# Layer 0's output projection: half of its contraction by seven block products for two outputs at a time

## The chip, the cores and the metric

The kernel runs on one core of a Trainium2 chip. The metric is the device time of one execution in microseconds (us); lower is better. The times are those of the executions that were timed, and beside them stands one profiled execution, whose trace gives every row quoted here.

TensorE (PE in the rows) multiplies a 128x128 block of weights with a moving tile and adds into PSUM; the loads of weights have rows of their own (PEld). VectorE (DVE) and ScalarE (ACT) work on SBUF and PSUM. SyncE (SP) issues most of the DMAs, GpSimd (POOL) those that add to their destination.

## The reference, cut to what matters

One step of a two-layer trunk in float32 over 576 tokens (512 of a prompt, 64 of samples), model width 1024 and branch width 2048. Layer 0 is a gated short convolution:

```python
def short_conv_mixer(h, buf, w_in, conv_w, w_out):
    b_gate, c_gate, xa, z = jnp.split(h @ w_in, 4, axis=-1)
    u = c_gate * xa
    conv, new_buf = causal_dwconv(u, buf, conv_w)
    y = b_gate * conv * jax.nn.silu(z)
    return y @ w_out, new_buf
...
    x = x + out
```

The change concerns `y @ w_out` of layer 0, a contraction over 2048 to 1024 outputs, and the residual sum. Layer 1 (an mLSTM block with the same kind of output projection) and the final norm come after it.

## The kernel before, in words

Everything is kept transposed: an activation is a tile of 128 features by 576 tokens, so the model width is 8 such tiles (`KD`) and the branch width 16 (`NW`). The precision of float32 is kept by splitting: `split` (L162) makes from a tile a high part (a cast by ScalarE) and a low part (a subtraction by VectorE), and each product of a 128x128 weight block with a tile is three matmuls, high by high, high by low and low by high.

**Two ways to multiply.** The plain way, `gemm` (L252) over `products` and `step`, runs for each of 8 blocks of weights three matmuls over two pieces of the tokens, 256 and 320 wide (L235). One output over a contraction of 2048 is two chunks of weights: 2 x 8 x 3 x 2 = 96 matmuls.

The other way, `block_pair` (L325), takes two outputs over a contraction of 1024 as a 2x2 block product: the two outputs are the rows, the even and odd feature tiles the inner blocks, the two halves of the tokens (288 each, `HT`) the columns. It uses a scheme of Strassen's kind with seven products in place of eight. Each product is 4 pairs of feature tiles by 3 matmuls of 288 columns (L345), so a pair of outputs takes 7 x 12 = 84 matmuls, where the plain way takes 96. The inputs must be there as sums and differences of the halves: `forms` (L283, with `mixed`, L268) makes them from two feature tiles, in four subtractions and additions of half a tile and three and a half splits. The weights must be there as sums too: `block_weights` (L302) loads two chunks (`r1`, `r2`), and in layer 0 lets DMAs build two of the sums: `s1` is loaded by SP and then added to by a POOL DMA, and one block of `r1` is added onto `r2`; VectorE makes the third sum in two steps (L354 and L350). `parts_of` (L258) splits each of the seven weight blocks, 128x512, one cast on ScalarE (L264) and one subtraction on VectorE (L265); four buffers each for high and low parts let it run up to three products ahead. Some products go through ScalarE copies out of PSUM on their way (L357, L362, L365, L375).

`plain` (L425) is the plain way in the two token halves of a block pair, 8 x 3 x 2 = 48 matmuls for a chunk. Layer 1 uses `gemm_pair` (L440) for its value projection: seven block products for one half of the contraction, then `plain` for the other half of both outputs, into the same PSUM banks.

**Layer 0.** The loop over `f` (L606 to L666) makes the 16 tiles of the branch: two block pairs for each `f` from 2 on, the convolution and gates on VectorE, and at its end `split` of the result into `ya` (L664). Then come the eight outputs of the output projection (L674 to L681): `gemm` over both chunks, the residual tile `x` loaded by SP and added from PSUM, its store, the scaled split for layer 1 (`h2`) and the sum of squares.

**What orders the work.** The kernel is written for a tile framework: code order gives priorities, and a scheduler with a timeline of its own fixes the order on each engine at build time. Each engine then runs its queue in order. Tiles of one tag share a fixed number of slots: 70 for the activation tiles (`T`), 4 for raw weight chunks, 7 for the scratch tiles of layer 0 (`X`, L108: the sums `s1` and `s2`, and `pu` and `m5` of a block pair, and some convolution inputs), 4 PSUM banks for the blocks of pairs.

## Time and profile before

| | us |
|---|---|
| median of 3 executions (1655.06 to 1657.25) | 1655.9 |
| span of the profiled execution, first to last instruction | 1654.3 |
| PE busy | 1627.4 (98%) |
| PE's weight loads busy | 1548.7 (94%) |
| DVE busy | 1125.8 (68%) |
| ACT busy | 806.9 (49%) |
| POOL busy | 148.8 (9%) |

The profiled execution's own time is its span of 1654.3 us and the little that lies around it. The other three executions were only timed, so the 1.6 us between span and median is taken as what lies around a span. In the rows a time is in us from the start of the span. A row of the timeline gives start, length, engine, line of the code, operation, output and inputs, and in brackets the time that the engine sat idle before it with the instruction that ended the wait. A row of the stretches gives, for a window, the busy time and the number of instructions of each engine, TensorE's granted clock (1.00 is full), the busy share of the DMA engines and GB/s.

Layer 0's loop ends and its output projection begins near 375 us; the last of the eight residual sums is at 479 us.

### The profile page before, as it was taken

The page shows a single profiled execution, that of the slowest core. Times are in us where ns is not written, and L with a number is a line of the kernel's source. Part 1 is how long each engine was busy: PE and PEld are TensorE (multiplying, and loading weights), DVE is VectorE, ACT ScalarE, POOL GpSimd, SP SyncE. Part 2 cuts the span into 40 slices and gives each one's busy share as a digit, 9 for nine tenths or more (in the row PEclk, how much of TensorE's full clock was granted, in tenths as well). Part 3 has the DMA queues.
Part 4 walks back from the last instruction along what each step waited for, and adds up shares of the span by engine and source line. Part 5 has one row for each costly group of instructions (what it writes and reads, how often), then busy time and mean ns, then how long its engine had stood idle before and what let it go on. Part 6 is the DMA issues. An engine that isn't in the chain of part 4 may idle for free. (4 is left out here: it accounts for less than half of the span.)

```text
span 1654.3 us, 31177 instructions
## 1 busy us (share of the span) xinstructions
PE 1627.4 (98%) x12029; PEld 1548.7 (94%) x12029; DVE 1125.8 (68%) x2124; ACT 806.9 (49%) x1622; POOL 148.8 (9%) x295
## 2 busy tenths in 40 slices
PE   9999999999999999999999999999999998999998
PEld 9999999999999999999899989899898787989997
DVE  7988898885337976555966456446458658688775
ACT  5566666653324553434645344344345456556431
POOL 1111111110001000000111010110101000000000
PEclk9999999999999999999999999999999899999999
DMA  6476666654332434535434554454556587998992
GB/s 219 111 174 167 175 168 159 175 136 148 120 120 91 149 121 128 172 119 159 156 103 151 156 177 162 142 188 140 173 190 241 186 280 262 336 341 296 359 342 103
DMA packets 121893, 301.61 MB, mean 182 GB/s; under 512 B 12656, under 2 KB 35056, under 8 KB 121744
## 3 DMA queue, kind: packets, MB, share of 16 engines
q1 hardware_dynamic: 98320, 267.61, 48.7%
q0 software_dynamic: 8064, 14.68, 5.8%
q10 hardware_dynamic: 15360, 17.32, 3.1%
q8 instruction: 94, 1.54, 0.4%
q14 instruction: 55, 0.45, 0.1%
HBM read 235.91 MB, written 63.66 MB: 181 GB/s over the span
## 5 line engine op out<-in xcount | busy, mean ns | idle before, releaser
L345 PE MATMUL p<-hi,wh 128*128 128x288 f32 x1540 | 454.4, 297 | 3.9 <-ACT p L357 1.9
L345 PE MATMUL p<-lo,wh 128*128 128x288 f32 x1540 | 452.6, 294 | 0.0
L345 PE MATMUL p<-hi,wl 128*128 128x288 f32 x1540 | 450.7, 295 | 0.2 <-DVE wl L265 0.2
L345 PEld LDWEIGHTS p<-hi,wh 128*128 128x128 f32 x1540 | 288.5, 188 | 12.7 <-DVE ws L350 4.1
L345 PEld LDWEIGHTS p<-lo,wh 128*128 128x128 f32 x1540 | 289.0, 188 | 0.0
L345 PEld LDWEIGHTS p<-hi,wl 128*128 128x128 f32 x1540 | 287.9, 188 | 0.4 <-DVE wl L265 0.4
L264 ACT CAST wh<-wr 128x512 fp32r<-128x512 f32 (+1 forms) x298 | 171.4, 578 | 215.4 <-PE p L345 123.5
L265 DVE TENSOR_TENSOR wl<-wr,wh 128x512 fp32r<-128x512 f32 (+1 forms) x298 | 185.0, 635 | 94.9 <-ACT wh L264 92.5
L235 PE MATMUL acc<-hi,wh 128*128 128x256 f32 (+1 forms) x1072 | 233.4, 298 | 1.8 <-ACT xm L711 1.0
L235 PE MATMUL acc<-lo,wh 128*128 128x256 f32 (+1 forms) x1072 | 231.9, 297 | 0.0
L235 PE MATMUL acc<-hi,wl 128*128 128x256 f32 (+1 forms) x1072 | 231.7, 297 | 0.0
L264 ACT CAST wh<-ws 128x512 fp32r<-128x512 f32 (+1 forms) x201 | 114.8, 573 | 203.8 <-PE p L345 129.6
L215 ACT CAST wh<-wr 128x512 fp32r<-128x512 f32 x170 | 104.7, 619 | 201.2 <-PE acc L235 148.1
L235 PEld LDWEIGHTS acc<-hi,wh 128*128 128x128 f32 x1072 | 180.4, 190 | 7.4 <-issue 1.6
L216 DVE TENSOR_TENSOR wl<-wr,wh 128x512 fp32r<-128x512 f32 x170 | 116.7, 689 | 98.7 <-ACT wh L215 88.6
L235 PEld LDWEIGHTS acc<-hi,wl 128*128 128x128 f32 x1072 | 179.9, 190 | 1.6 <-issue 1.3
L235 PEld LDWEIGHTS acc<-lo,wh 128*128 128x128 f32 x1072 | 179.9, 190 | 0.6 <-issue 0.2
L265 DVE TENSOR_TENSOR wl<-ws,wh 128x512 fp32r<-128x512 f32 (+1 forms) x201 | 125.5, 630 | 68.7 <-ACT wh L264 68.0
L1236 DVE SCALAR_TENSOR_TENSOR c<-c,cols,r 128x512 f32<-128x512 f32 x128 | 91.5, 743 | 27.0 <-PE r L1235 24.9
L433 PE MATMUL p<-hi,wh 128*128 128x288 f32 x496 | 109.2, 300 | 0.0
L433 PE MATMUL p<-hi,wl 128*128 128x288 f32 x496 | 107.3, 295 | 0.0
L433 PE MATMUL p<-lo,wh 128*128 128x288 f32 x496 | 107.0, 295 | 0.0
(388 smaller groups left out, 2619.1 us busy)
## 6 DMA issues: line engine op xcount, KB each, us to landing
wr<-wts SPq DMA_DIRECT2D x222, 512.0 KB, 3.6
c<-cs SPq DMA_DIRECT2D x112, 512.0 KB, 5.8
cs_out<-c SPq DMA_DIRECT2D x64, 512.0 KB, 7.5
ws<-wts SPq DMA_DIRECT2D x28, 256.0 KB, 4.5
ws<-wts POOLq DMA_DIRECT2D x28, 256.0 KB, 4.7
wr<-wts POOLq DMA_DIRECT2D x28, 256.0 KB, 4.1
x<-xcs SPq DMA_DIRECT2D x20, 288.0 KB, 4.8
x<-xT SPq DMA_DIRECT2D x16, 288.0 KB, 4.3
```

The costliest lines, as they stand in the source:

```text
L215: last_act[0] = nc.scalar.copy(hi, raw[:, 4 * i:4 * i + 4, :]).ins
L216: nc.vector.tensor_tensor(lo, raw[:, 4 * i:4 * i + 4, :], hi.bitcast(F32), ALU.subtract)
L235: nc.tensor.matmul(acc[:, o:o + j - i], a[:, k % 4, :], x[:, i:j], start=(first and k == 0 and p == 0), stop=(last and k == 7 and p == 2))
L264: last_act[0] = nc.scalar.copy(hi, src).ins
L265: nc.vector.tensor_tensor(lo, src, hi.bitcast(F32), ALU.subtract)
L345: nc.tensor.matmul(bank_, a[:, j, :], x, start=(start and n + j + i == 0), stop=(n == len(groups) - 1 and j == len(g) - 1 and i == 2), ski ...
L433: nc.tensor.matmul(b, a[:, k % 4, :], x[:, t:t + HT], start=bool(start) and k == 0 and i == 0, stop=(k == n - 1 and i == 2), skip_group_ch ...
L1236: ins = nc.vector.scalar_tensor_tensor(ct[:, j, :], ct[:, j, :], dec[:, o + j:o + j + 1], r, ALU.mult, ALU.add).ins
```

## The change

The two halves of the projection's contraction change places in the weight array, so that an even chunk (64, 66, ...) now belongs to the tiles `ya[8]` to `ya[15]` and an odd one (65, 67, ...) to `ya[0]` to `ya[7]`; the even chunks are stored with their blocks in the order that the block products want. The tiles 8 to 15 are no longer split; they become four `forms`, the first made within the loop after `f == 12`, the other three between the first plain products. The projection then runs so:

1. the weights of the first pair of outputs are requested (`block_weights(64, 66)`);
2. for outputs 0 to 3, `plain_onto`: the plain half over `ya[0:8]`, 48 matmuls each, added to the residual tile;
3. the seven products for outputs 0 and 1, then for 2 and 3, added onto these tiles (the existing `add` path of `block_pair`);
4. for outputs 4 and 5, then 6 and 7, `gemm_pair` with the new `onto`: seven products, then the plain half of each output into the same banks, then the sums onto the residual tile.

Each pair requests the weights of the next one (`then`). The opening of layer 1's buffers (`load_buffers("C", "states1", 2)`) and the end of layer 0's way of making weight sums (`layer0[0] = False`) move behind the projection.

```diff
@@ block_pair @@
+            if onto:
+                tt(o12, o12, u, ALU.subtract)
+                plain(bx, bw, c1 + 1, xs, None)
+                tt(o11, bx, o11, ALU.add)
+                tt(o12, bw, o12, ALU.add)
+                tt(o22, o22, m5, ALU.subtract)
+                plain(by, bv, c2 + 1, xs, None)
+                tt(o21, by, o21, ALU.add)
+                tt(o22, bv, o22, ALU.add)
+                return
...
+        def plain_onto(chunk, xs, o):
+
+            ba, bb = block(), block()
+            plain(ba, bb, chunk, xs, True)
+            for b, t in ((ba, 0), (bb, HT)):
+                nc.vector.tensor_tensor(o[:, t:t + HT], b, o[:, t:t + HT], ALU.add)
...
-            ya.append(split(cv))
+            ya.append(split(cv) if f < 8 else cv)
+            if f in (12,):
+                fy.append(forms(ya[8], ya[9]))
...
-        load_buffers("C", "states1", 2)
-        layer0[0] = False
...
-        for m in range(KD):
-            acc = gemm(64 + 2 * m, 2, ya)
+        block_weights(64, 66)
+        firsts = []
+        for m in range(4):
             x = T(name="x")
             load(out=x, in_=io["xT"][m])
-            nc.vector.tensor_tensor(x, flat(acc), x, ALU.add)
-            store(out=x1s[m], in_=x)
-            h2.append(split(x, col("norm1", m)))
-            sumsq(ssq, x, m == 0)
+            firsts.append(x)
+            plain_onto(65 + 2 * m, ya[0:8], x)
+            if m < 3:
+                fy.append(forms(ya[10 + 2 * m], ya[11 + 2 * m]))
+        for m in range(0, KD, 2):
+            c1, c2 = 64 + 2 * m, 66 + 2 * m
+            then = (c1 + 4, c2 + 4) if m < KD - 2 else None
+            if m < 4:
+                pair = firsts[m:m + 2]
+                groups, _ = ahead_of.pop((c1, c2))
+                block_pair(c1, c2, fy, None, *pair, True, then=then, groups=groups)
+            else:
+                pair = [T(name="x") for _ in range(2)]
+                for i, x in enumerate(pair):
+                    load(out=x, in_=io["xT"][m + i])
+                gemm_pair(c1, c2, fy, ya[0:8], *pair, then=then, onto=True)
+            for i, x in enumerate(pair):
+                store(out=x1s[m + i], in_=x)
+                h2.append(split(x, col("norm1", m + i)))
+                sumsq(ssq, x, m + i == 0)
+        load_buffers("C", "states1", 2)
+        layer0[0] = False
...
+    aout = _chunks(f["a_w_out"][0])[:, ::-1]
...
+    blk = [c for c in range(8, 64) if c % 4 < 2 or c // 4 in SECOND] + list(range(64, 80, 2))
```

## The prediction

> **What bounds the kernel now.** First the page's table of engines.

> ```profile
> span 1654.3 us, 31177 instructions
> PE 1627.4 (98%) x12029; PEld 1548.7 (94%) x12029; DVE 1125.8 (68%) x2124; ACT 806.9 (49%) x1622; POOL 148.8 (9%) x295
> ```

> TensorE is busy nearly all the time. So the question is whether it is so in the changed stage as well; three stretches answer that: the projection, the loop before it, and layer 1's value projection, which has the form that the last two pairs will have.

> ```profile
> 376.60:479.00 102.40, 102.40 (x770) 102.40 (x769) 42.23 (x63) 31.19 (x51) 0.00 (x0) 1.00 0.40 133
> 100.00:360.00 260.00, 260.00 (x1966) 260.00 (x1965) 228.36 (x399) 164.46 (x339) 44.72 (x57) 1.00 0.68 168
> 600.00:780.00 180.00, 180.00 (x1383) 176.35 (x1382) 104.29 (x183) 79.27 (x153) 12.52 (x28) 1.00 0.44 137
> ```

> PE has no idle time in any of them and the full clock. In the projection DVE is 41% busy; in the loop of block pairs 88%, and still PE never waits for it. The waits of TensorE between 340 and 640 us are these three:

> ```profile
> PE p L345 <- ACT wh L264: 1.2, 1, 1.2
> PE acc L235 <- ACT xm L711: 1.0, 1, 1.0
> PE p L345 <- DVE wl L265: 0.2, 1, 0.2
> ```

> The first and third belong to the loop's last pair, the second to layer 1's start. The stage is bound by TensorE, and a matmul less is worth its issue time until a wait takes its place.

> **What the change removes.** Today an output ends every 12.80 us, 96 matmuls: the first and last of the eight residual sums are 89.60 us apart, seven intervals.

> ```profile
> 389.61 0.76 DVE L678 TENSOR_TENSOR x<-acc,x 128x576 f32<-128x576 f32 x1 [2.12 <-PE acc L235]
> ...
> 479.21 0.76 DVE L678 TENSOR_TENSOR x<-acc,x 128x576 f32<-128x576 f32 x1 [2.08 <-PE acc L235]
> ```

> Eight outputs are 102.4 us. The price of a block pair's matmul comes from the loop: L357 runs once a pair, after its first product.

> ```profile
> 97.22 0.39 ACT L357 ACTIVATE p<-p 128x288 f32<-128x288 f32 x1
> ...
> 208.42 0.40 ACT L357 ACTIVATE p<-p 128x288 f32<-128x288 f32 x1
> ```

> These are ten pairs apart: 11.12 us a pair, 84 matmuls, 0.1324 us each (0.1333 in the plain way). The new stage has 4 x 84 = 336 in products and 8 x 48 = 384 in plain halves, 720 for 768. At 0.1324 that is 95.3 us: **-7.1 us**. [...]

> **VectorE's added work.** What counts is the distance of two starts:

> ```profile
> 337.55 0.69 DVE L354 TENSOR_TENSOR ws<-ws,wr 128x512 f32<-128x512 f32 x1
> 338.16 0.69 DVE L265 TENSOR_TENSOR wl<-wr,wh 128x512 fp32r<-128x512 f32 x1
> ...
> 502.72 0.45 DVE L271 TENSOR_TENSOR fa<-xm 128x288 f32<-128x288 f32 x1
> ...
> 506.85 0.45 DVE L288 TENSOR_TENSOR hl<-xm,hl 128x288 fp32r<-128x288 f32 x1
> 507.22 0.75 DVE L167 TENSOR_TENSOR lo<-xm,hi 128x576 fp32r<-128x576 f32 x1
> 507.88 0.75 DVE L709 TENSOR_TENSOR xm<-acc,rb 128x576 f32<-128x576 f32 x1
> ```

> A half tile takes 0.37 us to the next start, 512 columns about 0.60, a whole tile about 0.67; the lengths are 0.45, 0.69 and 0.75. A form is five half tiles and three whole ones: 3.86 us.

> In the loop one form is added behind f = 12, and the split of a tile (0.67) saved from f = 8 on. DVE's free share there, 12% of an f of 22.24 us, is 2.7 us, with the saving 3.4; 0.5 us runs over into the next f. I cost it at nothing: the weight splits run three products ahead, 4.8 us. Without that cover it costs 0.5.

> During the four plain halves (192 matmuls, 25.4 us) DVE has the rest of f = 15 (seven whole tiles, two halves: 5.4), eight weight splits (4.8), eight sums from PSUM (3.0) and three forms (11.6): 24.8 us. That just fits. During a pair that adds (11.1 us) it has seven weight splits, two weight sums, six half tiles and, for the pair before, four whole tiles: 4.2 + 1.2 + 2.2 + 2.7 = 10.3. It fits as tightly as in the loop. The last two pairs (23.8 us each) leave it room: 11 splits, 2 sums, 8 halves, 4 wholes are 13.4 us. ScalarE is below it throughout.

> **The waits that the change adds.** They have prices in rows elsewhere.

> (a) From plain halves to block products. Layer 1 has such a place:

> ```profile
> 812.21 0.40 PE L345 MATMUL p<-hi,wh 128*128 128x288 f32 x1 [1.95 <-ACT p L357]
> ...
> 823.91 0.40 PE L345 MATMUL p<-hl,wh 128*128 128x288 f32 x1 [0.68 <-DVE hl L288]
> ...
> 810.36 0.40 ACT L264 CAST wh<-wr 128x256 fp32r<-128x256 f32 x1 [2.68 <-DMA wr<-wts]
> ```

> It lost 2.6 us, of which 1.95 behind a late weight load that the new place does not have (its weights are asked for 25 us ahead); 0.7 is a form that came late. Bounds 0 and 2.6; I take 1.0, near the form's part, since DVE is 98% filled up to there. A gain is excluded: PE has no idle time there now.

> (b) A pair whose weights are asked for only within the pair before it. The loop's last pair is such:

> ```profile
> 355.78 0.40 ACT L362 COPY m<-p 128x288 f32<-128x288 f32 x1 [0.80 <-PE p L345]
> ...
> 357.07 0.42 SPq L311 DMA_DIRECT2D ws<-wts  x1
> ...
> 361.72 0.86 POOL L312 DMA_DIRECT2D ws<-wts  x1 [8.59 <-DMA ws<-wts]
> ...
> 365.84 0.62 ACT L264 CAST wh<-ws 128x512 fp32r<-128x512 f32 x1 [3.00 <-DMA ws<-wts]
> ...
> 366.51 0.40 PE L345 MATMUL p<-hi,wh 128*128 128x288 f32 x1 [1.24 <-ACT wh L264]
> 367.24 0.40 PE L345 MATMUL p<-hi,wl 128*128 128x288 f32 x1 [0.20 <-DVE wl L265]
> ```

> `s1` comes after `m5` in the code's order of `X` slots. From the copy of `m5` to `s1` with its addition landed were 10.0 us, and PE lost 1.44. In the new pairs for outputs 0/1 and 2/3 `m5` is copied 24 matmuls (3.2 us) into the pair; 10.0 and a cast of 0.62 later is 13.8, and PE runs dry after 84 + 12 matmuls, 12.7: 1.1 lost. But above, another load went out between copy and `s1`, which cost about 0.9 of the ten; without it nearly all is covered. Bounds 0 and 1.44; I take 0.6 each, 1.2 for the two. The step from 4/5 to 6/7 has 96 plain matmuls between and costs nothing.

> (c) The first plain chunk. Its slot is freed by the loop's last pair; there a load went out at 369.87:

> ```profile
> 369.87 3.43 SPq L221 DMA_DIRECT2D wr<-wts  x2
> ...
> 375.02 0.43 PE L235 MATMUL acc<-hi,wh 128*128 128x256 f32 x2
> ...
> wr<-wts SPq DMA_DIRECT2D x222, 512.0 KB, 3.6
> ...
> x<-xT SPq DMA_DIRECT2D x16, 288.0 KB, 4.3
> ```

> With 3.6 us and a cast it is ready at 374.1, and PE wants it at 375.0. Bounds 0 and 1.0, taken 0.3. On SP the three requests of the first pair stand ahead of it; two go out at 356 to 359 as loads do now.

> (d) PSUM banks and the end: a pair with plain halves holds all four banks, and the next pair's third bank is freed by two half-tile sums (0.74) 12 matmuls (1.6) ahead of its use. Layer 1's form of this shows no idle time (the third stretch). The last output's sums, scale and split, about 2.7 us, lie behind 42 matmuls (5.6) of layer 1's first product that do not need it. Taken 0.3, bounds 0 and 1.0. Moving the opening of layer 1's buffers costs nothing: a first use is the weight sums ahead of the value projection, some 70 us later.

> **The sum.** -7.1 + 1.0 + 1.2 + 0.3 + 0.3 = -4.3 us. The span would be 1650.0 and the median, 1.6 above a span as now, 1651.6.

> **Rivals.** First, **the weight chain in full**: both steps of (b) cost 1.44. For it: 512 KB loads of the pair after next may start in those very microseconds. Against: the DMAs are 40% busy there, 68% in the loop. -4.3 + 1.7 = -2.6: 1653.3.

> Second, **VectorE bound**: an operation costs its length, not the distance of starts. Then the plain halves hold 6.2 + 5.5 + 3.6 + 13.5 = 28.8 us of DVE (3.4 over) and an adding pair 11.9 (0.8 over, twice): 5.0 us in place of the 1.0 of (a), -0.3 in all: 1655.6. Against it are the rows above, which start before the one ahead ends; for it, a chain within a form that waits for ScalarE's casts. [...]

> Third, on the other side, **the residual tile's load as a link of a chain**. Slots of `T` seem to be given in code order: today each load of `x` is issued just behind the last tile of the output before.

> ```profile
> 391.09 0.67 ACT L460 ACTIVATE ssq<-x 128x576 f32<-128x576 f32 x1
> ...
> 403.89 0.67 ACT L463 ACTIVATE sq<-x 128x576 f32<-128x576 f32 x1
> ...
> 391.42 0.40 SPq L677 DMA_DIRECT2D x<-xT  x1
> ...
> 404.21 0.41 SPq L677 DMA_DIRECT2D x<-xT  x1
> ...
> 384.44 0.76 DVE L167 TENSOR_TENSOR lo<-cv,hi 128x576 fp32r<-128x576 f32 x1
> ```

> So `x` of outputs 1 to 3 waits for a form each. If DVE's queue holds the sum of an output ahead of the next form, a link is a form (502.72 to 507.97, 5.25), a load (4.3) and two sums (0.74): 10.3 us, against 6.4 of matmuls. Three links from the end of f = 15 (the last row, 385) reach 415.9, while the second product of the first pair wants a third bank. That is at 376.8 (the first residual sum's 389.61 less 12.80) + 25.4 + 1.6 = 403.8: 12.1 us lost in place of 1.0. +6.8: 1662.7. It decides from where a link is longer than the plain half. Against: forms are ready before the sums and can come ahead of them; and with the first at 378, beside f = 15, the loss is 5.1, no change in all.

> **Chances.** My forecast 0.62, the weight chain 0.15, VectorE 0.13, the chain of loads 0.10. A measurement of this kernel can tell about 0.2%, 3.3 us, from no change, so "faster" is below 1652.6. My forecast's own range, with all waits at zero (1648.8) or two of them near their upper bounds (1653.6), lies mostly below that: faster 0.56. The same takes its upper part, most of the first rival and the second: 0.32. Slower, the third and a little of the second: 0.12. The range, 1648.6 to 1656.6, takes in all but the third rival and a rest.

> **What would show it.** 48 matmuls fewer, and from the first plain matmul to layer 1's first 97 to 98.5 us in place of 102.4. PE waits on L264 of about half a microsecond at the second and third pair for (b), 1 us at the first pair's first products for (a), behind L288 or L265. VectorE above 90% busy through the plain halves with PE waiting on L265 would be the second rival; residual sums that wait for `x<-xT`, the third. I am wrong if the stage saves less than 3 us without one of these waits, or if the time is lost outside it.

## The result and the profile after

The changed kernel took 1660.87 us (median of 5 runs, 1658.45 to 1664.47) against 1655.90 us: a ratio of 1.0033 [1.0022, 1.0044]. The forecast, 1651.6 with a range to 1656.6, was wrong. Eleven later runs of the same kernel gave 1657.68 us and 1.0006 [0.9995, 1.0017]. The two intervals do not overlap, so an interval does not cover all that differs between two sets of runs. The kernel is slower by 1 to 5 us, and the 4.3 us that were forecast as a gain are not there. The profiled run is the fastest of the five, 1658.45 us. Of the runs below, one each of s3 and s4 took far longer (3561 and 1884 us); the ratios and mean clocks leave them out.

```profile
span 1656.5 us, 31247 instructions
PE 1627.4 (98%) x11981; PEld 1546.7 (93%) x11981; DVE 1152.0 (70%) x2192; ACT 821.9 (50%) x1658; POOL 154.8 (9%) x303
```

The 48 matmuls are gone (12029 before), and TensorE is busy just as long. Next the stage, from the first plain matmul to layer 1's first, and its first 25.8 us (columns: stretch, its length, busy time of PE, PEld, DVE, ACT, POOL, then the granted clock):

```profile
377.99:478.75 100.76, 98.60 (x723) 97.43 (x721) 69.06 (x124) 48.25 (x90) 5.20 (x6) 0.98 0.54 159
378.00:403.80 25.80, 25.77 (x194) 25.53 (x193) 23.01 (x45) 12.60 (x23) 0.86 (x1) 1.00 0.47 146
```

100.8 us where 97 to 98.5 were forecast, and it begins 1.4 us later than the old stage did. A landmark that all kernels share, VectorE's first `fa` of layer 1, stands nearly where it stood (502.72 before):

```profile
502.46 0.45 DVE L271 TENSOR_TENSOR fa<-xm 128x288 f32<-128x288 f32 x1
```

So in this profile 0.3 of the 7.1 us saved is left at this point. TensorE's waits from 300 to 480 us (total, times, longest) say where it went:

```profile
PE p L345 <- ACT wh L264: 2.8, 3, 1.7
PE p L345 <- DVE wl L265: 0.8, 2, 0.6
PE p L345 <- ACT p L357: 0.3, 1, 0.3
PE p L345 <- ACT pu L375: 0.2, 1, 0.2
```

The largest, 1.7, is a single stop, and its chain can be read in the timeline:

```profile
419.07 0.78 ACT L169 ACTIVATE hi<-x,cols 128x576 fp32r<-128x576 f32 x1 [0.93 <-DVE x L395]
419.76 0.38 ACT L362 COPY m<-p 128x288 f32<-128x288 f32 x1
...
420.09 0.45 SPq L311 DMA_DIRECT2D ws<-wts  x1
...
424.48 0.87 POOL L312 DMA_DIRECT2D ws<-wts  x1 [8.76 <-DMA ws<-wts]
...
428.04 0.29 PE L345 MATMUL p<-hi,wl 128*128 128x288 f32 x1
...
429.32 0.62 ACT L264 CAST wh<-ws 128x512 fp32r<-128x512 f32 x1 [3.09 <-DMA ws<-wts]
...
429.99 0.40 PE L345 MATMUL p<-hi,wh 128*128 128x288 f32 x1 [1.66 <-ACT wh L264]
...
430.82 0.40 PE L345 MATMUL p<-hi,wh 128*128 128x288 f32 x1 [0.30 <-ACT wh L264]
```

The copy of `m5` frees the slot of `s1`, SyncE loads, GpSimd adds, ScalarE casts, TensorE goes on. Counted by the matmuls ahead of it this is the pair for outputs 4/5. Matmuls start 0.13 us apart where nothing is late; by that measure 2.8 us are lost from 428.0 to 431.5 (that all waits on L264 from 300 to 480 us add up to 2.8 as well is a coincidence). What follows shows in windows of 3.4 us:

```profile
428.60:432.00 3.40, 1.71 (x8) 1.25 (x9) 2.73 (x5) 2.49 (x5) 0.00 (x0) 1.00 0.52 79
432.00:435.40 3.40, 3.40 (x17) 3.40 (x16) 3.32 (x7) 1.76 (x3) 0.00 (x0) 0.50 0.59 180
435.40:438.80 3.40, 3.40 (x27) 3.40 (x27) 2.24 (x5) 1.44 (x3) 0.32 (x1) 0.99 0.88 311
```

PE is busy half of the first; in the second its clock is halved, with 17 matmuls in place of 27, 0.24 us apart: 1.5 us more. PE's busy time does not show that loss, only the clock and the count do.

### The profile page after: what moved, and what is told of

Same layout as the page of the kernel before. It is cut to its first block, busy times and chain, and to the rows that moved or that the text cites. A ratio compares the mean times of both kernels' runs of the same rounds, so it can differ in the third digit from the quotient of the medians.

```text
span 1656.5 us, 31247 instructions
## 1 busy us (share of the span) xinstructions
PE 1627.4 (98%) x11981; PEld 1546.7 (93%) x11981; DVE 1152.0 (70%) x2192; ACT 821.9 (50%) x1658; POOL 154.8 (9%) x303
## 5 line engine op out<-in xcount | busy, mean ns | idle before, releaser
L345 PE MATMUL p<-hi,wh 128*128 128x288 f32 x1636 | 483.6, 297 | 5.1 <-ACT wh L264 2.8
L345 PE MATMUL p<-lo,wh 128*128 128x288 f32 x1636 | 481.5, 295 | 0.0
L345 PE MATMUL p<-hi,wl 128*128 128x288 f32 x1636 | 478.2, 295 | 0.8 <-DVE wl L265 0.8
L345 PEld LDWEIGHTS p<-hi,wh 128*128 128x128 f32 x1636 | 307.2, 188 | 15.0 <-DVE ws L350 4.1
L345 PEld LDWEIGHTS p<-lo,wh 128*128 128x128 f32 x1636 | 307.6, 188 | 0.0
L345 PEld LDWEIGHTS p<-hi,wl 128*128 128x128 f32 x1636 | 306.1, 188 | 1.3 <-DVE wl L265 1.2
L264 ACT CAST wh<-wr 128x512 fp32r<-128x512 f32 (+1 forms) x314 | 181.2, 579 | 224.7 <-PE p L345 120.5
L265 DVE TENSOR_TENSOR wl<-wr,wh 128x512 fp32r<-128x512 f32 (+1 forms) x314 | 195.7, 636 | 99.0 <-ACT wh L264 96.9
L264 ACT CAST wh<-ws 128x512 fp32r<-128x512 f32 (+1 forms) x213 | 122.3, 575 | 215.6 <-PE p L345 131.5
L265 DVE TENSOR_TENSOR wl<-ws,wh 128x512 fp32r<-128x512 f32 (+1 forms) x213 | 133.3, 631 | 70.7 <-ACT wh L264 70.0
L235 PE MATMUL acc<-hi,wh 128*128 128x256 f32 (+1 forms) x816 | 178.9, 300 | 1.6 <-ACT xm L747 1.3
L235 PE MATMUL acc<-lo,wh 128*128 128x256 f32 (+1 forms) x816 | 177.5, 298 | 0.0
L235 PE MATMUL acc<-hi,wl 128*128 128x256 f32 (+1 forms) x816 | 177.1, 298 | 0.0
L235 PEld LDWEIGHTS acc<-hi,wh 128*128 128x128 f32 x816 | 137.7, 190 | 7.1 <-issue 1.6
L235 PEld LDWEIGHTS acc<-hi,wl 128*128 128x128 f32 x816 | 137.1, 190 | 1.6 <-issue 1.3
L235 PEld LDWEIGHTS acc<-lo,wh 128*128 128x128 f32 x816 | 137.2, 190 | 0.6 <-issue 0.2
L443 PE MATMUL p<-hi,wh 128*128 128x288 f32 x560 | 122.9, 299 | 0.0
L443 PE MATMUL p<-hi,wl 128*128 128x288 f32 x560 | 121.0, 295 | 0.0
L443 PE MATMUL p<-lo,wh 128*128 128x288 f32 x560 | 120.8, 295 | 0.0
## 6 DMA issues: line engine op xcount, KB each, us to landing
wr<-wts SPq DMA_DIRECT2D x222, 512.0 KB, 3.6
c<-cs SPq DMA_DIRECT2D x112, 512.0 KB, 5.8
cs_out<-c SPq DMA_DIRECT2D x64, 512.0 KB, 7.2
x<-xcs SPq DMA_DIRECT2D x20, 288.0 KB, 4.8
x<-xT SPq DMA_DIRECT2D x16, 288.0 KB, 4.1
```

The source lines that it names most:

```text
L235: nc.tensor.matmul(acc[:, o:o + j - i], a[:, k % 4, :], x[:, i:j], start=(first and k == 0 and p == 0), stop=(last and k == 7 and p == 2))
L264: last_act[0] = nc.scalar.copy(hi, src).ins
L265: nc.vector.tensor_tensor(lo, src, hi.bitcast(F32), ALU.subtract)
L345: nc.tensor.matmul(bank_, a[:, j, :], x, start=(start and n + j + i == 0), stop=(n == len(groups) - 1 and j == len(g) - 1 and i == 2), ski ...
L443: nc.tensor.matmul(b, a[:, k % 4, :], x[:, t:t + HT], start=bool(start) and k == 0 and i == 0, stop=(k == n - 1 and i == 2), skip_group_ch ...
```

## The experiments

`fa` is the start of the landmark in the run's profile, the clock is the mean of the granted clock over the timed runs. The kernel before had clocks of 0.993 to 0.994 and medians of 1655.3 to 1656.7.

| run | ratio to before | median us | clock | `fa` |
|---|---|---|---|---|
| changed | 1.0033 [1.0022, 1.0044] | 1660.87 | 0.9900 | 502.46 |
| e1_ahead | 0.9991 [0.9982, 1.0000] | 1654.57 | 0.9931 | 499.36 |
| e2_drop | 0.9970 [0.9959, 0.9981] | 1650.94 | 0.9934 | 497.09 |
| e3_order | 1.0012 [1.0003, 1.0021] | 1657.62 | 0.9928 | 504.70 |
| e4_before_order | 1.0048 [1.0034, 1.0062] | 1662.51 | 0.9924 | 505.65 |
| e5_ahead_order | 0.9981 [0.9972, 0.9990] | 1653.29 | 0.9942 | 500.09 |
| e6_form_before_plain | 1.0059 [1.0046, 1.0072] | 1665.92 | 0.9910 | 509.85 |
| e7_busy_wait | 1.0002 [0.9993, 1.0010] | 1656.80 | 0.9939 | 503.55 |
| e8_ahead_forms_between | 1.0002 [0.9992, 1.0012] | 1657.06 | 0.9923 | 501.11 |
| e9_busy_old_tail | 1.0018 [1.0009, 1.0027] | 1658.95 | 0.9920 | 504.07 |
| e10_ahead_old_tail | 0.9991 [0.9982, 1.0000] | 1654.33 | 0.9934 | 498.18 |
| e11_all | 0.9988 [0.9979, 0.9997] | 1653.69 | 0.9935 | 502.14 |
| e12_form_at_11 | 1.0014 [1.0002, 1.0026] | 1658.23 | 0.9920 | 503.92 |
| s1_stop_new_order | 1.0013 [1.0004, 1.0022] | 1657.72 | 0.9922 | 503.50 |
| s2_stop_old_order | 1.0003 [0.9994, 1.0012] | 1657.21 | 0.9931 | 504.62 |
| s3_ahead_new_order | 0.9984 [0.9975, 0.9993] | 1653.38 | 0.9930 | 499.08 |
| s4_ahead_old_order | 0.9985 [0.9976, 0.9994] | 1653.57 | 0.9936 | 500.11 |
| s5_changed_again | 1.0006 [0.9995, 1.0017] | 1657.68 | 0.9917 | 505.04 |
| s6_before_new_order | 1.0026 [1.0015, 1.0036] | 1660.92 | 0.9932 | 505.88 |

`fa` comes from one profile each, and it moves between profiles of one kernel: s5 is the changed kernel again, and its `fa` is 2.6 us later. The difference arises at the stop of the loop's last pair, which every kernel here has. In s5 it falls into one window, and a halved one follows (first two rows); in the changed kernel's first profile it falls across two, and none follows (last two):

```profile
366.30:369.70 3.40, 1.39 (x9) 0.96 (x8) 2.62 (x6) 2.57 (x6) 0.46 (x1) 1.00 0.60 79
369.70:373.10 3.40, 3.40 (x16) 3.40 (x16) 3.40 (x8) 1.88 (x5) 0.12 (x1) 0.50 0.17 53
```

```profile
363.70:367.10 3.40, 2.68 (x21) 2.45 (x19) 1.46 (x4) 1.41 (x4) 0.88 (x1) 1.00 0.86 124
367.10:370.50 3.40, 3.00 (x21) 2.80 (x22) 3.40 (x7) 3.28 (x8) 0.58 (x1) 1.00 0.16 27
```

Counted by the starts of the matmuls, 4.0 us are lost there in s5 and 1.6 in the first profile. The profiles of e8, e9, e11 and e12 have this halved window too (368.6 to 370.4 us), so their `fa` is about 2 us late for a reason that is not in their edit.

**The first four** set two theories against each other: A, the projection's stop; B, late layer 1, whose instructions the build puts into another order after the change although its code is the same.

e1 asks for a block pair's weights one pair earlier:

```
+        block_weights(68, 70)
         for m in range(0, KD, 2):
-            then = (c1 + 4, c2 + 4) if m < KD - 2 else None
+            then = (c1 + 8, c2 + 8) if m < KD - 4 else None
```

> The changed kernel, with the weights of outputs 2/3 requested ahead of the first pair's products and those of 4/5 within the first pair, so each pair's weights are asked for one pair earlier. Theory A (the gain was eaten in the projection by the wait for s1 at outputs 2/3, 2.8 us, and the half-clock window of 3.4 us behind it, 1.6 us): both go, the projection is 4.3 us shorter, layer 1 starts that much earlier, and the median falls by about 4, to near 1656.5. Theory B (most of the 5 us is lost in layer 1's late part, because the build put its instructions into another order): the projection is shorter all the same, but the late part of layer 1 is ordered in yet another way and the total can be anything from 1652 to 1662.

The stop and the half clock are gone (the places called outputs 2/3 here are 4/5), and `fa` is 3.1 us earlier than in the changed kernel, where theory A had 4.3; the median fell further than it had (1654.57, not 1656.5). Of the 2.8 us of waits on L264 only the old one of the loop's last pair is left:

```profile
PE p L345 <- ACT wh L264: 1.1, 1, 1.1
PE p L345 <- DVE wl L265: 0.6, 1, 0.6
```

e2 is the kernel before without each output's last contraction block, which its results would need:

```
             for c_ in range(nchunk):
+                if c_ == 1:
+                    w = weights(chunk0 + c_)
+                    for k in range(7):
...
+                    continue
                 products(acc, weights(chunk0 + c_), xs[8 * c_:8 * c_ + 8], c_ == 0, c_ == nchunk - 1, pops)
```

> The kernel before, with 48 of the projection's 768 plain matmuls left out (the last block of the contraction, six matmuls for each output): only the work that the change saves, none of its machinery. In layer 1's second half its instructions stand nearly as in the kernel before (2 rows of SyncE's queue differ, 10 of VectorE's). Both theories: -6.4 us at layer 1's start. Theory A: -6.4 at the end too, 1649.5. Theory B: -6.4 as well, since the order is nearly kept, give or take 1. If the end gains less than 4, late layer 1 takes time back for a reason that is neither the order nor the waits.

Its landmark is 5.6 us earlier than before, its median 5.0: 48 matmuls are worth nearly their issue time (6.4 us at 0.1333). Counted from the projection's first matmul (375.02 before, 375.79 in e2) to `fa` it is 127.7 and 121.3 us, the whole 6.4; so the saving itself is real.

e3 and e4 add matmuls whose results nobody reads, to the changed kernel (12) and to the kernel before (16); by them the build swaps the order of late layer 1:

```
+for i in range(12):
+    nc.tensor.matmul(block("fill"), ya[0][0][:, 0:P], ya[0][0][:, 0:HT], start=True, stop=True)
```

> The changed kernel with 12 more matmuls at the projection's end, whose results nothing reads (1.6 us of TensorE). With them the build orders layer 1's second half as in the kernel before (2 rows of TensorE and VectorE differ, none of SyncE and ScalarE; in the changed kernel 85, 48, 12 and 16). Theory B: late layer 1 gives back the 3.5 us that it lost in the profile, so the total falls by about 2 to 3.5 although work was added: 1657.5 to 1659. Theory A: +1.6, 1662.5.

> The kernel before with 16 more matmuls at the projection's end, whose results nothing reads (2.1 us of TensorE). With them the build orders layer 1's second half as in the changed kernel (3 rows of TensorE differ, 2 of ScalarE, none of VectorE and SyncE). Theory B: +2.1 for the matmuls and +3.5 or more in late layer 1, 1661 to 1663. Theory A: +2.1 alone, 1658.

Both moved as B has it: e3 came out 3.3 us below the changed kernel's five runs in spite of more work, e4 6.6 us above the kernel before, with 2.9 of it there at `fa`. Taken alone they would have made B the main cause.

**The next four** took the parts together, and asked what sets off the half clock.

e5 is e1 with 16 fillers of 64 columns, which restore the old order:

> The first experiment's kernel (weights of a block pair asked for one pair earlier) with 16 short matmuls of 64 columns behind the projection, whose results nobody reads. With them the build orders layer 1's second half as it does in the kernel before. Theories A and B both true and independent: the wait for s1 (2.8 us) and the half clock behind it (1.6) are gone, and so is the loss of late layer 1 (4.5); the fillers cost at most 16 x 0.06 = 1 us, likelier 0.5. 1660.9 - 4.4 - 4.5 + 0.5 = 1652.5, range 1651 to 1654; no wait of PE for kst of L1174. If the order alone does not matter and the first experiment's 1654.6 is all there is, 1655 to 1656. If late layer 1 loses whatever it gets ahead of time, since it waits for something else, also about 1655.

1653.29: as both theories added up had it, and faster than both kernels. Its 0.06 us a filler was the author's estimate, which no run shows; in the two by two below eight more of them go with 1.0 and 1.1 us at `fa`.

e6 moves `fy.append(forms(ya[8], ya[9]))` out of the loop to just ahead of the first plain chunk:

> The changed kernel, with the form of outputs 8 and 9 made just ahead of the first plain chunk and not in the loop behind f = 12. Late layer 1 stays in the changed kernel's order, so whole times compare directly. Theory: the stop of 0.9 us at 334 us (PE behind wl) comes from VectorE being filled to the brim by that form, and goes; a little may come back where the plain halves end, at 404 us, since VectorE has one form more there. Projection start earlier by 0.9, layer 1's start earlier by 0 to 0.9; whole time 1660.0, range 1659 to 1661. Rival: the stop at 334 belongs to the loop and stays, and the form on the other side makes a new wait of about 2 us at 404; 1662 to 1663.

A miss by 6 us. The stop at 334 us goes, but VectorE falls behind, and the weights' chain with it (waits 300 to 480 us of e6):

```profile
PE p L345 <- ACT wh L264: 5.5, 4, 3.2
PE p L345 <- ACT p L357: 0.9, 1, 0.9
PE p L345 <- DVE hl L288: 0.8, 1, 0.8
PE p L345 <- DVE wl L265: 0.8, 1, 0.8
```

The rival's 2 us at 404 us came true. The stop of 3.2 us is, counted by the matmuls ahead of it, at outputs 2/3, where the changed kernel lost 0.5; and halved windows start at 407.8 and 424.9 us.

e7 puts 15 matmuls into the stop:

```
 bw = block("p5")
+for i in range(15 * (c1 == 72)):
+    nc.tensor.matmul(bw, ya[0][0][:, 0:P], ya[0][0][:, 0:HT], start=True, stop=True)
 product(bw, s1, "t1", True)
```

> The changed kernel with 15 matmuls of 288 columns put into the wait for s1 (c1 == 72, ahead of its first product with s1), into a bank that this product overwrites: TensorE works 2.0 us where it stood idle, and the wait for the weights stays as long. The build orders late layer 1 as in the kernel before. Theory: the half clock behind the wait is set off by the idle time; it goes, and layer 1 starts 1.5 us earlier than in the changed kernel. With late layer 1 in the old order (4.5): 1660.9 - 1.5 - 4.5 = 1654.9, range 1653.5 to 1656. Rival: the half clock comes from something else that happens there (the DMA load, the end of the pair): it stays, layer 1 starts at the changed kernel's time, 1656.4, range 1656 to 1658.

```profile
428.60:432.00 3.40, 3.15 (x23) 2.70 (x22) 2.20 (x4) 2.14 (x5) 0.00 (x0) 1.00 0.62 104
432.00:435.40 3.40, 3.40 (x26) 3.39 (x27) 3.40 (x7) 2.08 (x4) 0.00 (x0) 1.00 0.42 116
```

With the stop filled, the clock stays whole: it was the idle time that set off this half clock. The time, 1656.80, lies outside the range all the same, where the rival had it, for layer 1 did not start earlier (`fa` 503.55): a wait of 1.1 us for the plain chunk's cast came up at 440 us, which the slow matmuls had covered.

e8 is e1 with all four forms between the plain chunks:

> Candidate without fillers: weights of a block pair asked for one pair earlier, as in the first experiment, and all four forms made between the plain chunks (none in the loop), one behind each of the four. The build then orders late layer 1 nearly as in the kernel before. Gains against the changed kernel: 4.4 (the wait and the half clock), 0.9 (the stop at 334 us), 4.0 to 4.5 (late layer 1). Price: the last form stands behind the fourth plain chunk; if VectorE works it off in time 0, if not up to a form, 3.9 us, of wait at 404 us, taken 1.5. 1660.9 - 4.4 - 0.9 - 4.3 + 1.5 = 1652.8, range 1651 to 1655. If late layer 1's order does not matter: 1656 to 1657.

A miss by 4: 1.9 us are lost where the plain halves end (1.3 of it for `hl` of L288), more than the 0.9 of the loop that it saves, and its clock is low. In its profile about 2 us more go to the halved window at 369.4; what the other runs lost isn't explained.

**Then the order with less around it.** e9 is e7 with 10 fillers, e10 is e1 with the form at f = 11, e11 is e10 with 14 fillers of 64 columns, e12 the changed kernel with the form at f = 11:

> As the seventh experiment, but with 10 matmuls in the wait for s1 and not 15; with ten the build leaves late layer 1 in the changed kernel's order. (That wait stands at outputs 4/5, counted by the matmuls ahead of it; the expectations so far called it outputs 2/3.) Theory C, from the profiles so far: the granted clock is halved for 3.41 us after each window of 3.41 us, on a grid that runs by itself, in which the array worked less than about 0.4 of the time; the change loses by such windows, one in the projection (1.5 us) and, since the build put late layer 1 into an order in which TensorE waits 1.7 us for kst at 1422 us, more of them there. Then here the window of the projection is gone (work in its place 0.28 + 10 x 0.12 / 3.41 = 0.63) and those of late layer 1 stay: 1660.9 - 1.5 = 1659.4, range 1658 to 1660.5; mean granted clock 0.991; the wait for kst of L1174, 1.5 to 1.7 us, is there. If the order has no part in it, the time is that of the seventh experiment, 1656.8, range 1655.5 to 1658, and the clock 0.994.

> The first experiment's kernel (weights of a block pair asked for one pair earlier), with the loop's one form made behind f = 11 and not f = 12; with it the build orders late layer 1 exactly as in the changed kernel. It differs from the fifth experiment's kernel in late layer 1's order, in that form's place (0.5 us either way) and in the 16 short fillers (0.5). Theory C, the order costs 3 to 4.5 us by its wait for kst and the half clocks around: 1653.3 + 3.5 = 1656.8, range 1655.5 to 1658.5, with a clock of 0.992; layer 1 starts 2.5 to 3.4 us earlier than before. If the loss of late layer 1 was tied to the projection's stop and not to the order: 1652.5 to 1654, clock 0.994.

> The tenth experiment's kernel with 14 matmuls of 64 columns behind the projection, whose results nobody reads; with them the build orders late layer 1 as in the kernel before. Nothing else differs. Theory C: the changed order costs 2.6 us in the tenth (its layer 1 was 3.8 us ahead of the kernel before at 1300 us, its median only 0.9), the fillers 0.4: its ratio to the kernel before falls from 0.9991 to 0.9978, range 0.997 to 0.9985, 1651 to 1653.5 us; clock 0.994 on the mean of the runs; no wait for kst of 1 us or more. If the order has no part in it: ratio 0.999 to 1.0, 1654 to 1655.5.

> The changed kernel with the loop's one form made behind f = 11 and not f = 12; late layer 1 stays in the changed kernel's order. Theory C: the stop of 0.9 us at 334 us goes, as in the tenth experiment, the stop of 2.8 us at outputs 4/5 stays, with a halved clock behind it where it fills enough of one window, and late layer 1 loses about as the changed kernel did, by the wait for kst and half clocks: 1660.9 - 0.9 = 1660.0, range 1658 to 1661.5; clock of the runs 0.990 to 0.992. If the form's place sets what the rest loses: 1656 to 1658.

e9 and e12 fit (both expectations start from 1660.9); e10 came out 2.5 us below what C expected, and e11 only 0.6 below e10, outside its range: the order costs less than C had it. e9's 0.12 us of work a matmul was the author's estimate and is not shown: in both profiles matmuls of 288 columns start 0.132 us apart (median, at the full clock), and by that the window would be 0.31 + 0.39 = 0.70 filled. The wait for `kst` is where the new order is, and absent with the old one. In the changed kernel it is followed by a halved clock (the wait and two windows, first fence), in e10 it falls across two windows and is not (second):

```profile
PE pn L1210 <- DVE kst L1174: 1.7, 1, 1.7
1421.90:1425.30 3.40, 1.66 (x13) 1.41 (x12) 3.40 (x7) 2.83 (x7) 0.00 (x0) 1.00 1.06 318
1425.30:1428.70 3.40, 3.40 (x15) 3.16 (x14) 3.40 (x9) 2.49 (x5) 0.36 (x2) 0.50 1.01 404
```

```profile
1416.20:1419.60 3.40, 2.96 (x23) 2.75 (x21) 3.16 (x7) 3.40 (x9) 0.00 (x0) 1.00 1.03 335
1419.60:1423.00 3.40, 2.33 (x15) 2.06 (x16) 3.40 (x8) 2.83 (x5) 0.36 (x2) 1.00 1.03 399
1423.00:1426.40 3.40, 3.40 (x27) 3.36 (x26) 3.33 (x12) 1.68 (x4) 0.00 (x0) 1.00 1.02 414
```

The wait itself comes from SyncE's queue. In the kernel before (first fence) the loads of the values go out 2.7 us earlier than in the changed kernel (second), which has a load of `c` and one of `kps` swapped ahead of them; the casts of the values and then `kst` follow.

```profile
1404.62 6.77 SPq L1147 DMA_DIRECT2D ld<-vps  x4
...
1414.85 0.19 ACT L1255 CAST vh<-cst 128x2 fp32r<-128x2 f32 x1 [0.63 <-DMA ld<-vps]
```

```profile
1407.32 3.78 SPq L1183 DMA_DIRECT2D ld<-vps  x4
...
1416.78 0.19 ACT L1291 CAST vh<-cst 128x2 fp32r<-128x2 f32 x1 [2.81 <-DMA ld<-vps]
```

**A two by two on one chip** to settle the sizes: stop or none (weights asked for earlier), new or old order (8 or 16 fillers of 64 columns):

> Two by two, all four on one chip. This one: the changed kernel with 8 matmuls of 64 columns behind the projection (results unread); stop at outputs 4/5 as in the changed kernel, late layer 1 in the changed kernel's order (new order). Theory C: like the changed kernel, 1.0033 of the kernel before; range 1.0015 to 1.004; granted clock 0.990 to 0.992 on the mean of the runs.

> As the one before, with 16 short matmuls and not 8, by which the build puts late layer 1 into the order of the kernel before (old order). The 8 more cost at most 0.5 us. Theory C (the order costs 2.6 us on the mean, by a wait for kst and the halved clocks it sets off): 1.0015 of the kernel before, at least 0.0010 below the run with the new order, clock 0.002 higher. If the order costs nothing: the same ratio as that run, or 0.0003 above it.

> The first experiment's kernel (weights of a block pair asked for one pair earlier, so no stop at outputs 4/5) with 8 matmuls of 64 columns; late layer 1 in the new order. Theory A (the stop and the half clock behind it cost 4 us in all): 0.0024 below the changed kernel with 8, about 1.0005. Theory C for the order: 0.0016 above the next run.

> The fifth experiment's kernel again: weights asked for one pair earlier, 16 short matmuls, late layer 1 in the old order. It had 0.9981; expected 0.9975 to 0.9990. Both theories: below each of the other three; 0.0024 below the second, 0.0016 below the third. If the order costs nothing: equal to the third.

All but s4 came out below the ratios expected, which start from the changed kernel's 1.0033. The stop costs 0.0029 (s1 less s3) and 0.0018 (s2 less s4), 4.8 and 3.0 us, and 4.4 and 4.5 at `fa`, in these rows of s1 and s3:

```profile
503.50 0.45 DVE L271 TENSOR_TENSOR fa<-xm 128x288 f32<-128x288 f32 x1
```

```profile
499.08 0.45 DVE L271 TENSOR_TENSOR fa<-xm 128x288 f32<-128x288 f32 x1
```

That is the stop's 2.8 and the half clock's 1.5. Theory A holds, with its size. The order comes to 0.0010 with the stop and nothing without it (s3 and s4 should have differed by 0.0016). With the eight further fillers `fa` is 1.1 and 1.0 us later; net of that the order is 1.7 + 1.1 = 2.8 us and -0.2 + 1.0 = 0.8 us. By the intervals each difference of two ratios is uncertain by about 0.0013, 2 us: the stop's cost is clear of that, the order's is not.

> The changed kernel once more, unchanged, with more runs than the five it has. Its five gave 1.0033 [1.0022, 1.0044], its near twin with 8 short matmuls 1.0013 [1.0004, 1.0022]. If the five runs fell high by chance: about 1.0018, range 1.001 to 1.0025, mean clock 0.992. If something is particular to this build: 1.003 or more, clock 0.990.

> The kernel before with 20 matmuls of 64 columns behind its projection (results unread, at most 1 us), by which the build puts late layer 1 into the changed kernel's order. It stands to the kernel before as the fourth experiment's did, with less work in the fillers. If the new order costs what the two by two shows, 0 to 1.7 us: 1.0003 to 1.0015. Theory B, 4.5 us: 1.003 or more.

s5, the changed kernel again, came out below its range: the five runs had fallen high. s6 has the new order, and nothing of the changed projection: 4.3 us above the kernel before by its ratio, 3.2 of them at `fa` already (by one profile), so 1.1 for the order. e7 and e9, on different chips, differ by 2.6, and e4, by five runs, has 7.9 - 2.9 = 5.0. Theory B's 4.5 us has fallen as the main cause; the pairs with ten runs or more give the order 0.8 to 2.8 us, always of the same sign, and its exact size stays open. That e5, e9 and e12 fitted was luck in part: their sums start from 1660.9, which s5 puts at 1657.7, and e5's takes off 4.5 for the order.

## Why the prediction was wrong, step by step

- **What bounds the stage, and the 7.1 us**: right in the main. From the first plain matmul to `fa` the kernel before takes 126.1 us (127.7 less the 12 matmuls of the loop that come behind that first one), the changed kernel 124.5; with the stop taken away e1 takes 120.2 and e10 119.5. So 5.9 to 6.6 of the 7.1 are there once the stop is not.
- **(a) the handover, 1.0**: nothing was lost. The first block product starts in step with the last plain matmul:

```profile
403.58 0.43 PE L443 MATMUL blk<-hi,wl 128*128 128x288 f32 x2
403.85 0.42 PE L345 MATMUL p<-hl,wh 128*128 128x288 f32 x2
```

- **(b) weights asked for within the pair before, 0.6 twice: the step that failed.** At outputs 2/3 it cost 0.5; at 4/5 2.8, and 1.5 of half clock behind it: 4.8 in place of 1.2. The prediction had the copy of `m5` 3.2 us into the pair, straight behind its product, and 9.5 us from there until PE runs dry. The product ended at 418.7 and the copy came at 419.76, as ScalarE had the cast of the output before (L169) ahead of it, which waited for VectorE's L395: 8.4 us until PE ran dry at 428.2. The chain itself was 9.6 from the copy to the cast's start, near the 10.0 of the loop's last pair and not the 9.1 that the prediction hoped for without the other load. That pair, from which price and upper bound were taken, has no such cast in its way; and its 1.44 counts idle time alone, where the starts of its matmuls show 2.0 us lost. That a stop may halve the clock afterwards was in no term and no rival.
- **(c) 0.3**: 0.3. **(d) 0.3**: no stop for banks; layer 1's wait for `xm`, 4 us behind `fa`, grew from 1.0 to 1.3.
- **The loop's form, costed at nothing, 0.5 if its cover is gone**: the cover is gone, at 0.9. VectorE was at its limit in the loop (busy 14.0 of the 14.0 us from 320 to 334, 13.2 before), and TensorE waits for `wl` (e6, without that form, has no such stop):

```profile
333.97 0.29 PE L345 MATMUL p<-lo,wh 128*128 128x288 f32 x1
334.87 0.40 PE L345 MATMUL p<-hi,wl 128*128 128x288 f32 x1 [0.60 <-DVE wl L265]
```

- **Not in the sum**: 0.6 us at 374 us, in the loop's last pair, behind the copy of L375. e6 and e8 have it too, so it isn't the form's; its cause wasn't pursued.
- **The rivals**: the weight chain in full was the right mechanism at one of its two places, and larger than its bound of 1.44. VectorE's length per operation and the chain of residual loads are out: 23.0 of 25.8 us of VectorE in the plain halves, and no stop at their end.
- **Outside the stage** the sum held no term. The build reordered late layer 1, which costs about 1 to 3 us by the pairs above, each uncertain by 2. The prediction named "lost outside it" as what would prove it wrong; part of it was.

Added up at `fa`: -7.1 + 0.5 + 4.3 + 0.9 + 0.6 + 0.3 = -0.5 (-0.3 measured in this profile). In s5, with the further halved window at 369.7, `fa` is 2.3 us behind the kernel before.

## What to carry to other kernels

Price a weight load that is asked for when a slot comes free by everything queued on the engine that frees it, not by the transfer alone; and where the sum shows less than a microsecond of room, ask one stage earlier: here two lines turned a kernel at 1.0006 to 1.0033 into one at 0.9991, and at 0.9981 and 0.9985 with the old order restored. In the changed kernel a stop that lost 2.8 us cost 1.5 us on top, as a halved clock followed it. Differences of 2 us between builds are judged by ten runs or more and in pairs that share their instruction order, for an edit in one stage may reorder another.
